# An attention chain beside projections: eight q buffers, the fourth q projection no longer behind all scores of the first key/value half, attention steps of 5.2

## The chip, the cores and the metric

One core of a Trainium2 chip runs the whole computation in one launch. The metric is the device time of that launch in microseconds (us). Engines: TensorE (PE, matmuls), VectorE (DVE), ScalarE (ACT), GpSimd (POOL), SyncE (SP, issues DMAs). Each engine runs its instructions in the order in which they are written, and waits on semaphores for the others.

## The reference

A two-layer encoder over 512 + 256 = 768 tokens of width 1024, all in fp32. Each layer is half a SwiGLU block, a mixer, half a SwiGLU block. The change lies in the mixer of layer 0, in short:

```
z = rmsnorm(x) @ w_in
u, vh = gelu(z[:, :1024]) split in two of 512
vh = layer_norm(vh)
vmix = per block of 128 tokens, per group of 128 columns: sgu_w[g] @ vh + sgu_b
a_out = u * vmix
q (8 heads of 64), k, v (2 heads of 64) = rest of z; rope on q and k
b_out = softmax over a window of 3 blocks of 128, with a sink, of q k^T / 8; times v
out = concat(a_out, b_out) @ w_out
```

Tokens of the two requests (4 and 2 blocks of 128) do not see each other. Four q heads share one k/v head.

## The kernel before, in words

Activations lie feature-major, in tiles of 128 features by 768 tokens, and every fp32 matmul is three passes: each operand is split into a high part (fp32r, ScalarE cast) and a low remainder (VectorE subtract, L115 for weights, L197 for activations), and TensorE adds high·high, high·low and low·high (`mm3`, L176). The mixer's tokens are worked on in two groups, 512 and 256 tokens wide (GROUPS). PSUM has four banks of the kind "mm" (projections) and four of the kind "aux" (attention, gate), each handed out in turn.

TensorE's order is written out by hand. The kernel keeps a model time `self.t` that each matmul advances by its nominal length. Side work is written as Python generators ("chains", `spawn`): a chain yields a gap, and is due again that much later in model time. After every `mm3`, `tick` steps the chains that are due, so side work is put between the matmuls of a projection. `run_until(cond)` (L164) is the other way to step them: it steps the chains in order of their due times, with no projection between, until the condition holds, moving the model time on. The orders of the other engines come from the framework's scheduler, which knows the dependences; it fixes them at build time.

In `mixer0` (L925), in the order of the code:

- the k and v projections, with rope tables and the split of k;
- the attention chain is spawned with the gap `GAP0` (L46);
- `q_heads(m)` for m = 0, 1, 2 (L996): each projects 128 q columns (two heads) in both groups, 8 `mm3` of 512 columns and 8 of 256, applies rope on VectorE (L960 to L963) and writes a high and a low tile for each group. Each group's tiles are taken from a ring of six buffers (tag q0, q1), that is, three calls' worth;
- `vh_part`: the gate half of the input projection, twice three blocks of 128 tokens, each 8 `mm3` of 512 columns. Each block's result goes through Gelu on ScalarE (L1119, which reads the PSUM bank) into a `sgu` chain: layer norm on VectorE (L1080, L1083, a reciprocal root in small integer and float steps L265 to L276, L1085, L1088, L1089), a split (vhh, vhl), then 12 small matmuls with the gate weights and an add (L1103);
- the line L1139, `self.run_until(lambda: (0, 5) in scored)`: the attention chain is stepped until it has issued the scores of half 0, block 5;
- `q_heads(3)`; the attention's half 1 needs q heads 2 and 3;
- `u_part` (L1121 and on): the u half, 4 times two groups, L1129, Gelu L1130, product L1133;
- `mixer_out`: the output projection; its operand tiles are split just ahead (oh on ScalarE L196, ol on VectorE L197).

The attention chain handles (half kv, block n) for kv = 0, 1 and n = 0 to 5. A round is: scores S of block n (12 matmuls; mask and row maximum on VectorE L905 and L909, exponentials on ScalarE L911, sink L915 to L917, reciprocal L918, scaling of p L920), a gap, values V of block n−1 (one pair of matmuls for each key block; moved out by L1049 and L1052), a gap, transposes T of p of block n (4 for each key block; split into th and tl), 0.3 of a gap. Blocks 0, 3, 4 and 5 have two key blocks, 1 and 2 three.

Weights come by DMA through four raw buffers (SP's queue), well ahead, and are split by ScalarE and VectorE.

Of the kernel before, what the change touches and what calls it, by code (L numbers as in the profile page):

```python
# [10 lines left out]
F32R = mybir.dt.float32r  # L11
# [5 lines left out]
P = 128  # L17
# [25 lines left out]

WTOTAL = 12 * D * FF + 8 * EARLY * P * D + D * 1792 + 2 * D * D + D * 3072 + D * 512
VTOK = (4.0,9.0)
GAP0 = 5.4  # L46
SGU = (8.0, 3.0, 4.0)
NP, NQ = 16, 2
GAPS1 = (3.5, 0.6, 3.5, 0.8)
# [2 lines left out]
class Trunk:  # L52
# [872 lines left out]
    def mixer0(self):  # L925
        nc = self.nc
        mp = self.mixer_open("m0")
# [29 lines left out]
        def roped(ps, c0, c1):  # L957
            n = c1 - c0
            t, u = tmp("rt")[:, :n], tmp("ru")[:, :n]
            nc.vector.stream_shuffle(out=u, in_=ps[:, :n], mask=swap)  # L960
            nc.vector.tensor_tensor(out=t, in0=ps[:, :n], in1=rct[:, c0:c1], op=ALU.mult)
            nc.vector.tensor_tensor(out=u, in0=u, in1=rst[:, c0:c1], op=ALU.mult)
            nc.vector.tensor_tensor(out=t, in0=t, in1=u, op=ALU.add)  # L963
            return t
# [18 lines left out]
        for g in (0, 1):  # L983
            c0, c1 = GROUPS[g]
# [11 lines left out]
        def q_heads(m):  # L996
            qs = []
            w = self.unit("l0_w_in", 0, KD, 1024 + m * P, P)
            for g in (0, 1):
                c0, c1 = GROUPS[g]  # L1000
                t = roped(self.proj(w, xs, GROUPS[g]), c0, c1)
                qs.append([mp.tile([P, c1 - c0], F32R, tag=f"q{g}", name=f"q{g}", bufs=6) for _ in "hl"])
                self.q_split(*qs[g], t)
            qheads.append(qs)

# [51 lines left out]
        qheads, scored, gates = [], [], []  # L1057

        def attention(gap):
            cur = None  # L1060
            for kv in (0, 1):
                for n in range(6):
                    while len(qheads) < 2 * kv + 2:
                        yield 0.5
                    new = score(kv, qheads[2 * kv : 2 * kv + 2], n)
                    scored.append((kv, n))
                    yield gap
                    if cur:
                        values(*cur[:3], tt)
                    yield gap  # L1070
                    cur = new
                    tt = turn(*cur)
                    yield 0.3 * gap
            yield 1.0
            values(*cur[:3], tt)
# [31 lines left out]
        def vh_part():  # L1107
            for n0 in (0, 3):
                ps = [self.psum() for _ in range(3)]
                for k in range(KD):  # L1110
                    if k % 2 == 0:
                        w = self.unit("l0_w_in", k, 2, 512, 512)
                    for i in range(3):
                        a, b = (n0 + i) * P, (n0 + i + 1) * P
                        st = (self.xh[k][:, a:b], self.xl[k][:, a:b])
                        self.mm3(ps[i], st, w[k % 2], k == 0, k == KD - 1)
                for i in range(3):
                    v = tmp("vg")
                    nc.scalar.activation(v, ps[i], AF.Gelu, scale=self.ry[:, n0 + i : n0 + i + 1])  # L1119
                    gates.append(self.spawn(sgu(n0 + i, v)))  # L1120
# [13 lines left out]

        att = self.spawn(attention(GAP0))
        for m in range(3):
            q_heads(m)
        vh_part()
        self.run_until(lambda: (0, 5) in scored)  # L1139
        q_heads(3)  # L1140
        u_part()
        self.mixer_out("l0_w_out", ot, att)
# [422 lines left out]
```

## Time and profile before

| | |
|---|---|
| median of 3 runs | 2632.54 us (2632.37 to 2633.5) |
| profiled execution, its own time | 2634.87 us |
| its span | 2633.1 us |
| its mean granted TensorE clock | 0.99 |
| first mixer in the span | about 535 to 740 us |

The profile is one execution. Its page gives busy times by engine, 40 slices of the span, and the chain of work that ended last. Further views are windows (busy time by engine and granted clock in each stretch), waits (what ended an engine's idle time, summed: total us, times, longest), and the timeline (start, duration, engine, line, operation, output<-inputs, shape; in brackets the idle time before it and what ended it). Matmuls are pipelined: their durations overlap, and the distance of their starts is what one costs.

### The profile page before, as it was taken

The numbers are of one execution on the slowest core, as the hardware profiler recorded it, in microseconds if no ns is written. First come the engines' busy times: TensorE is split into PE (matmuls) and PEld (weight loads), VectorE is DVE, ScalarE is ACT, GpSimd is POOL, SyncE is SP. The second block draws the span as 40 slices with busy tenths as digits, with TensorE's granted clock in tenths as the row PEclk, the third lists the DMA queues.
The fourth block names the chain that finished last, engine by engine and source line by source line (L and its number), as shares of the span: only waits on it lengthen the run. The fifth ranks groups of instructions, "written<-read, shape, count | busy, mean of one in ns | idle before, by whom it ended". The sixth has DMA issues, their size and how long they took to land.

```text
span 2633.1 us, 41175 instructions
## 1 busy us (share of the span) xinstructions
PE 2561.3 (97%) x15094; PEld 2491.3 (95%) x15094; DVE 2267.8 (86%) x4793; ACT 1365.6 (52%) x2851; POOL 88.0 (3%) x172
## 2 busy tenths in 40 slices
PE   7999999998999999999999999999999999999997
PEld 7999999987899999999999999989998989999997
DVE  8998889889779988898999888886777699988886
ACT  7544444555655544454654544454545465454443
POOL 0000000000100000000000000001222100000000
PEclk9999999999999999999999999999999999999998
DMA  5423222421223222222322222232221332222221
GB/s 168 133 78 103 71 81 65 145 87 37 89 77 97 81 81 77 68 75 86 96 81 81 73 73 74 88 111 63 63 63 40 105 104 81 81 71 74 68 87 54
DMA packets 83898, 218.99 MB, mean 83 GB/s; under 512 B 20080, under 2 KB 32880, under 8 KB 83696
## 3 DMA queue, kind: packets, MB, share of 16 engines
q1 hardware_dynamic: 83552, 216.34, 26.5%
q8 instruction: 118, 1.93, 0.3%
q14 instruction: 84, 0.69, 0.1%
q10 hardware_dynamic: 144, 0.03, 0.0%
HBM read 206.90 MB, written 15.07 MB: 84 GB/s over the span
## 4 chain that ended last, share of the span: by engine, by line
PE 86%; DVE 9%; ACT 2%; DMA 2%; issue 1%; SPq 0%; DVEq 0%; ACTq 0%
PE ps_mm L140 54%; PE ps_aux L140 31%; DMA raw<-in_w 1%; DVE wlo L115 1%; PE ps_aux L144 1%; DVE s L609 1%; DVE xl L739 1%; ACT p L911 1%; DVE p L920 0%; DVE p L905 0%; DVE tl L197 0%; ACT whi L114 0%; ACT xh L738 0%; DVE ol L197 0%; DVE x L706 0%
## 5 line engine op out<-in xcount | busy, mean ns | idle before, releaser
L114 ACT CAST whi<-s 128x512 fp32r<-128x512 f32 x496 | 304.9, 621 | 390.6 <-DVE s L609 133.1
L114 ACT CAST whi<-raw 128x512 fp32r<-128x512 f32 x512 | 311.0, 619 | 257.8 <-PE ps_mm L140 116.8
L115 DVE TENSOR_TENSOR wlo<-s,whi 128x512 fp32r<-128x512 f32 x496 | 337.0, 685 | 61.1 <-ACT whi L114 60.8
L115 DVE TENSOR_TENSOR wlo<-raw,whi 128x512 fp32r<-128x512 f32 x494 | 337.5, 691 | 28.3 <-ACT whi L114 24.1
L140 PE MATMUL ps_aux<-dt,whi 128*128 128x384 f32 x864 | 219.3, 334 | 2.1 <-ACT whi L114 2.1
L140 PE MATMUL ps_mm<-db,whi 128*128 128x384 f32 x864 | 219.2, 334 | 0.0
L140 PEld LDWEIGHTS ps_aux<-dt,whi 128*128 128x128 f32 x864 | 156.0, 188 | 2.4 <-ACT whi L114 2.4
L140 PEld LDWEIGHTS ps_mm<-db,whi 128*128 128x128 f32 x864 | 156.1, 188 | 0.0
L140 PE MATMUL ps_mm<-xh,whi 128*128 128x512 f32 (+1 forms) x416 | 147.4, 354 | 3.8 <-ACT xh L738 3.8
L140 PE MATMUL ps_aux<-dt,wlo 128*128 128x384 f32 x432 | 144.4, 334 | 0.3 <-DVE wlo L115 0.3
L140 PE MATMUL ps_mm<-db,wlo 128*128 128x384 f32 x432 | 144.4, 334 | 0.0
L140 PE MATMUL ps_mm<-xl,whi 128*128 128x512 f32 (+1 forms) x416 | 142.3, 342 | 1.1 <-DVE xl L739 1.1
L140 PE MATMUL ps_mm<-xh,wlo 128*128 128x512 f32 (+1 forms) x416 | 142.1, 341 | 0.0
L609 DVE TENSOR_TENSOR s<-raw 128x512 f32<-128x512 f32 x124 | 85.0, 686 | 23.0 <-DMA raw<-in_w 22.9
L499 DVE TENSOR_TENSOR u<-ps_aux,u 128x384 f32<-128x384 f32 x176 | 97.0, 551 | 2.8 <-PE ps_aux L140 2.6
L609 DVE TENSOR_TENSOR s<-raw,raw 128x512 f32<-128x512 f32 x124 | 83.7, 686 | 18.2 <-DMA raw<-in_w 18.0
L140 PE MATMUL ps_aux<-dh,whi 128*128 128x384 f32 x384 | 97.6, 335 | 0.6 <-DVE x L706 0.6
L911 ACT ACTIVATE p<-p,st 128x256 f32<-128x256 f32 (+3 forms) x144 | 68.9, 480 | 55.0 <-DVE st L909 54.9
L494 ACT COPY u<-ps_mm 128x384 f32<-128x384 f32 x176 | 83.5, 474 | 24.2 <-PE ps_mm L140 24.0
L661 DVE TENSOR_TENSOR x<-ps_aux,x 128x384 f32<-128x384 f32 x160 | 86.0, 552 | 9.3 <-PE ps_aux L140 9.2
L140 PEld LDWEIGHTS ps_mm<-xh,whi 128*128 128x128 f32 x416 | 79.9, 192 | 14.1 <-ACT xh L738 4.9
L140 PE MATMUL ps_mm<-oh,whi 128*128 128x384 f32 x256 | 88.1, 344 | 4.6 <-DVE x L888 4.0
(486 smaller groups left out, 8058.2 us busy)
## 6 DMA issues: line engine op xcount, KB each, us to landing
raw<-in_w SPq DMA_DIRECT2D x350, 512.0 KB, 3.7
xdm<-x SPq DMA_DIRECT2D x16, 384.0 KB, 2.3
x<-in_x SPq DMA_DIRECT2D x16, 192.0 KB, 5.5
x<-xdm SPq DMA_DIRECT2D x8, 384.0 KB, 3.4
xold<-xdm SPq DMA_DIRECT2D x8, 384.0 KB, 3.0
out_y<-y SPq DMA_DIRECT2D x8, 384.0 KB, 2.4
tab<-skew SPq DMA_DIRECT2D x8, 256.0 KB, 4.8
raw<-in_w SPq DMA_DIRECT2D x8, 256.0 KB, 2.6
```

The lines of the kernel that those rows point to most:

```text
L114: nc.scalar.copy(hi, src)
L115: (eng or nc.gpsimd).tensor_tensor(out=lo, in0=src, in1=hi.bitcast(F32), op=ALU.subtract)
L140: self.nc.tensor.matmul(out, lhsT=lhsT, rhs=rhs, start=start, stop=stop, **kw)
L144: self.nc.tensor.transpose(out, src, self.ident)
L494: nc.scalar.copy(e[n, out], bank[key, n])
L499: nc.vector.tensor_tensor(out=t, in0=bank[key, n], in1=t, op=ALU.add)
L609: f = lambda o, x, y, op: self.nc.vector.tensor_tensor(out=o, in0=x, in1=y, op=op)
L661: nc.vector.tensor_tensor(out=o, in0=ps, in1=o, op=ALU.add)
L739: nc.vector.scalar_tensor_tensor(out=lo, in0=src, scalar=gain, in1=hi.bitcast(F32), op0=ALU.mult, op1=ALU.subtract)
L911: nc.scalar.activation(outs[i], outs[i], AF.Exp, bias=nm[:, i : i + 1], accum_out=sm[:, i : i + 1])
```

## The change

Three edits, all for `mixer0`. Each attention step's gap is 5.2 instead of 5.4 model microseconds. The ring of q tiles has eight buffers for each group instead of six, so that the tiles of all four calls exist at once. The call of `run_until` ahead of `q_heads(3)` is gone, so that the fourth q projection follows the gate half directly, and the attention chain's steps fall between its matmuls and those of `u_part` as they come due.

```diff
-GAP0 = 5.4
+GAP0 = 5.2
...
-                qs.append([mp.tile([P, c1 - c0], F32R, tag=f"q{g}", name=f"q{g}", bufs=6) for _ in "hl"])
+                qs.append([mp.tile([P, c1 - c0], F32R, tag=f"q{g}", name=f"q{g}", bufs=8) for _ in "hl"])
...
         for m in range(3):
             q_heads(m)
         vh_part()
-        self.run_until(lambda: (0, 5) in scored)
         q_heads(3)
         u_part()
         self.mixer_out("l0_w_out", ot, att)
```

## The prediction

> **What bounds the kernel now.** I read the page first (busy times and the chain of waits), then the windows of the first mixer, then TensorE's waits there, then the timelines of TensorE, VectorE and ScalarE around the largest hole.
>
> ```profile
> span 2633.1 us, 41175 instructions
> PE 2561.3 (97%) x15094; PEld 2491.3 (95%) x15094; DVE 2267.8 (86%) x4793; ACT 1365.6 (52%) x2851; POOL 88.0 (3%) x172
> PE 86%; DVE 9%; ACT 2%; DMA 2%; issue 1%; SPq 0%; DVEq 0%; ACTq 0%
> ```
>
> TensorE carries the end: 97% busy, 86% of the chain. An edit that leaves its matmuls as they are can only move its idle time and the stretches that run at a low clock. VectorE at 86% is the only other engine near the path.
>
> The windows (columns: span, then busy time of PE, PEld, DVE, ACT, POOL, then the granted clock) show where in this mixer that time lies:
>
> ```profile
> 620.00:625.00 5.00, 0.18 (x1) 0.19 (x2) 5.00 (x38) 2.93 (x10) 0.00 (x0) 0.80 0.05 20
> 625.00:630.00 5.00, 3.91 (x20) 2.93 (x19) 5.00 (x13) 2.63 (x5) 0.00 (x0) 0.50 0.01 2
> 630.00:635.00 5.00, 5.00 (x22) 4.28 (x22) 4.88 (x28) 0.61 (x2) 0.00 (x0) 0.68 0.01 3
> 600.00:650.00 50.00, 41.87 (x252) 35.25 (x253) 48.44 (x191) 24.06 (x55) 0.00 (x0) 0.90 0.14 42
> 650.00:700.00 50.00, 48.67 (x296) 41.81 (x295) 38.93 (x114) 36.17 (x79) 2.58 (x2) 1.00 0.22 68
> ```
>
> TensorE does next to nothing from 620 to 625 and runs at a low clock until about 633, while VectorE is full. Behind 650 VectorE has 11 us of 50 to spare. The hole in the timeline:
>
> ```profile
> 617.56 0.39 PE L140 MATMUL ps_mm<-wlo,xh 128*128 128x512 f32 x1
> 617.79 0.39 PE L140 MATMUL ps_mm<-whi,xl 128*128 128x512 f32 x1
> ...
> 618.70 0.39 PE L140 MATMUL ps_aux<-tl,vt 128*128 128x512 f32 x1
> 624.82 2.03 PE L144 MATMUL ps_aux<-ident,p 128*128 128x128 f32 x8 [5.74 <-DVE p L920]
> ...
> 628.45 0.58 PE L140 MATMUL ps_aux<-kh,q 64*128 64x256 f32 x1 [1.09 <-DVE tl L197]
> ...
> 634.26 0.45 PE L140 MATMUL ps_mm<-xh,whi 128*128 128x512 f32 x1
> ...
> 645.06 0.28 PE L140 MATMUL ps_mm<-xh,whi 128*128 128x256 f32 x1
> 645.18 0.28 PE L140 MATMUL ps_mm<-xl,whi 128*128 128x256 f32 x1
> ```
>
> This is the place of the deleted line. Waiting for all scores of kv 0 lets the attention chain step with no projection between: values, transposes of block 4 (waiting 5.74 us for p), scores of block 5 (waiting 1.09 us for tl). At full clock a 512-column matmul follows the last by 0.23 us (617.56 to 617.79), a 256-column one by 0.12 (645.06 to 645.18). What holds p is VectorE's order, the gate's layer norm in front of it:
>
> ```profile
> 618.89 0.69 DVE L1080 BATCH_NORM_STATS2 bs<-vg 128x6 f32<-128x512 f32 x1
> ...
> 624.33 1.13 DVE L920 TENSOR_SCALAR p<-p,st 128x256 f32<-128x256 f32 x4
> ```
>
> **The change part by part.** The instructions are the same; their order differs. Durations come from the profiled execution (2634.87 us, span 2633.1), 2.3 us above the median of the runs, 2632.54; everything below is a difference inside that execution, and I add it to the median.
>
> *The wait that goes.* Between 619.09 (last matmul before the hole) and 634.26, 15.2 us, TensorE did 8 transposes, 12 score, 6 projection and 12 gate matmuls: 6 by 0.23 and 32 of at most 256 columns by 0.12 are 5.2 us at most, and about 4.7 since the score matmuls start in pairs. So 10.5 us are lost there (10.0 at least): 5.74 and 1.09 of waiting, the rest clock. Without the line the fourth q projection (24 matmuls of 512 columns by 0.23 and 24 of 256 by 0.12, 8.4 us) lies between the steps of blocks 4 and 5. Following the changed orders of both engines with the durations of before, I have p of block 4 ready at 629.2 and TensorE there at 631.8. −10.5 us. TensorE's other waits there (columns: total us, times, longest) are
>
> ```profile
> PE ps_aux L140 <- DVE vhl L197: 0.7, 2, 0.5
> PE ps_aux L140 <- DVE o L1103: 0.6, 1, 0.6
> ```
>
> and belong to the same stretch of the old order; what stands in their place is counted anew below: −1.3 us.
>
> *Eight q buffers.* The fourth projection would otherwise wait for the scores of kv 0 to release one of six; with eight it waits for none. It costs memory, no instruction: 0.
>
> *Steps of 5.2.* Each attention step issues one projection group (3 matmuls, 0.69 us) earlier. That changes ScalarE's order in the gate half. In the kernel before, all three gate Gelus come ahead of the exponentials:
>
> ```profile
> 586.28 0.69 ACT L1119 ACTIVATE vg<-ps_mm,sm 128x512 f32<-128x512 f32 x1
> 587.68 1.43 ACT L1119 ACTIVATE vg<-ps_mm,sm 128x512 f32<-128x512 f32 x2 [0.72 <-PE ps_mm L140]
> ...
> 589.64 1.28 ACT L911 ACT_TABLE_LOAD   x1
> 590.93 0.62 ACT L911 ACTIVATE p<-p,st 128x384 f32<-128x384 f32 x1
> ...
> 593.35 0.19 ACT L916 ACTIVATE st<-st 128x4 f32<-128x4 f32 x1
> ```
>
> In the changed order one gate Gelu comes, then a table load, four exponentials, another load, and only then the other two Gelus. The second of them frees the PSUM bank that TensorE takes at the matmul which now starts about
>
> ```profile
> 589.56 0.39 PE L140 MATMUL ps_mm<-whi,xh 128*128 128x512 f32 x1
> ```
>
> (same position in both orders). The first Gelu starts at 587.0 to 587.7 (behind its last matmul, which comes after the scores now), ends 0.7 later, then 1.28 for the load, 2.6 for exponentials and the sink's (590.93 to 593.54), 1.28 again, 0.7: 593.5 to 594.2. So TensorE waits 4.0 to 4.7 us where it waited nothing. Queued behind that matmul on TensorE are the values, the transposes and scores of block 3, all that feeds VectorE next.
>
> The next scores (block 3) then wait for tl of the transposes: in the changed VectorE order it stands behind the layer-norm steps of two gate blocks and reaches its end about 605.9, with TensorE there at 602 to 604, 2 to 4 us. The two waits replace lesser ones of before. Walking both engines with the row durations, TensorE ends the gate half at 623.3 instead of 618.0: +5.3 us.
>
> *The gate's mixing matmuls* of the second half now come beside the fourth q projection, whose rope work on VectorE is in front of their vhl. The first step of that rope is
>
> ```profile
> 642.96 0.74 DVE L960 STREAM_SHUFFLE ru<-ps_mm 128x512 f32<-128x512 f32 x1
> ```
>
> Four such steps and the q split for 512 columns are 3.1 us at some 0.62 each, and about half for 256. By the walk vhl of the first of two blocks is ready at 642.4 with TensorE there at 641.1, that of the next at 647.9 with TensorE at 645.1: 1.3 and 2.8 us, and a transpose bank of block 5 comes 0.7 late: +4.8 us.
>
> *Clock.* What a wait costs beyond itself:
>
> ```profile
> 2140.41 0.41 PE L140 MATMUL ps_mm<-b110h,whi 128*128 128x384 f32 x1 [2.70 <-DVE sg L508]
> 2142.00:2144.00 2.00, 2.00 (x8) 2.00 (x7) 1.45 (x4) 1.19 (x4) 0.00 (x0) 0.50 0.26 104
> 252.05 0.62 PE L140 MATMUL ps_aux<-dt,whi 128*128 128x384 f32 x2 [2.12 <-ACT whi L114]
> 254.00:256.00 2.00, 2.00 (x13) 2.00 (x12) 2.00 (x5) 0.07 (x1) 0.00 (x0) 1.00 0.00 0
> ```
>
> A wait of 2.70 is followed by a granted clock of 0.50 for about as long as the wait, so about half the wait again is lost; one of 2.12 leaves the clock at 1.00. The first new wait's clock loss falls into the second wait. The 2.8 at vhl sits on the edge: +1.3 us taken, 0 to 1.3. [...]
>
> *The end of the mixer.* The output projection follows the u projections; its operands oh and ol come two at a time, and the waits and casts of before are
>
> ```profile
> 690.41 0.38 PE L140 MATMUL ps_aux<-kh,q 64*128 64x256 f32 x1 [0.91 <-DVE tl L197]
> 701.24 0.44 PE L140 MATMUL ps_mm<-oh,whi 128*128 128x384 f32 x1 [0.58 <-ACT oh L196]
> 702.04 0.44 PE L140 MATMUL ps_mm<-ol,whi 128*128 128x384 f32 x1 [0.36 <-DVE ol L197]
> 691.97 2.58 ACT L196 CAST oh<-o 128x384 fp32r<-128x384 f32 x6 [0.54 <-PE ps_mm L140]
> 694.49 2.89 DVE L197 TENSOR_TENSOR ol<-o,oh 128x384 fp32r<-128x384 f32 x6
> ```
>
> 1.85 us, and with the shorter gaps around them about 3.0 in all. In the changed order the first output matmul waits for an ol behind more of the u product; then a pair of oh (0.43 each, 2.58 by 6) takes 0.86 and one of ol (0.48 each) 0.96 against some 0.51 for the three matmuls that use it (384 columns, 0.17 each between the two pitches above): I get 4.9 us lost, +2.0 (0 to 4). At the last values of the mixer, 45 matmuls (7.7 us) lie between them and their first reader, in the old order and the new; no cost. The weight loads on SP's queue keep their order, and none of them ends a wait of TensorE here: 0.
>
> *Table loads.* Before has 13 in this mixer (7, 4 and 2):
>
> ```profile
> L911 ACT ACT_TABLE_LOAD x7 | 9.0, 1283 | 0.1
> L1130 ACT ACT_TABLE_LOAD x4 | 5.1, 1283 | 0.1
> L1119 ACT ACT_TABLE_LOAD x2 | 2.6, 1283 | 0.0
> ```
>
> The changed order has 17. Four more by 1283 ns are 5.1 us on an engine that is about half busy; what of it is on the path is already in the walk of the gate half, the rest is hidden behind its idle time. [...]
>
> Sum: −10.5 −1.3 +5.3 +4.8 +1.3 +2.0 = +1.6 us, 2634. The bounds: with both waits of the gate half covered (0), those for vhl and their clock at half (3.1) and no loss at the end, −8.7: 2624. With the first wait's clock loss not covered by the second (+2) and the end at +4: 2638.
>
> **The rivals.** *Faster, 2624:* the hole goes and the new waits are mostly covered. For it: VectorE idles 11 us in 650 to 700, and the fourth projection is 8.4 us of work that doesn't need it at once. Against: VectorE is full from 620 to 630 and its work ahead of vhl isn't less. Price: the lower bounds above.
>
> *Slower, 2640:* ScalarE's switches starve VectorE. Between 600 and 650 VectorE idles 1.6 us; if the loads keep it from layer-norm statistics or p between 586 and 620, all that it owes later (p, tl, vhl) comes later by as much. Four loads of 1283 ns are 5.1 us, and with a half-clock stretch behind one wait of some 2.7 us (1.3) it is 2632.5 + 1.6 + 5.1 + 1.3 = 2640.5. It decides from about 3 us of VectorE idle in that stretch. For it: one Gelu stands ahead of each load. Against: before has VectorE full there with loads between too. [...]
>
> *Nothing moves, 2632.5:* VectorE's backlog to 650 sets the pace whatever TensorE's order; the hole is cut into pieces of the same sum.
>
> **How the numbers follow.** A measurement can tell about 0.2% (5.3 us) from no change: under 2627.3 is faster, above 2637.8 slower. My forecast gets 0.45 (of it 0.33 within, 0.05 faster, 0.07 slower), the faster rival 0.25 (0.22 beyond the bound, 0.03 within), the slower one 0.22 (all beyond), the one that moves nothing 0.08 (within). Faster 0.27, same 0.44, slower 0.29. The likeliest case alone ranges from 2628 to 2638; the range that takes in most of the rivals runs from 2622 to 2643.
>
> **What would show it.** Right: no TensorE wait over 1 us for p of block 4; a wait of 4 to 5 us near 590 for a PSUM bank held by ScalarE's Gelu, with a granted clock near 0.50 behind it; a wait for tl near 603; waits of 1 to 3 us for vhl near 642 and 647; 17 table loads. Wrong: no wait near 590 (then faster), or VectorE idle over 3 us from 586 to 620 (then slower), or the waits at the output projection more than 4 us above 3.0.

## The result and the profile after

The changed kernel takes 2638.86 us in the median of 18 runs (2635.36 to 2642.87), the kernel before 2634.22 in 18 (2631.38 to 2638.37) taken beside them. The ratio is 1.0019, with a 95% interval of 1.0012 to 1.0025: slower by 3 to 7 us, best 5.0. That lies inside the predicted range (2622 to 2643), above the forecast of 2634, and just within the 0.2% that the prediction called no change.

The page of the profiled execution after (2637.11 us) is nearly that of before: TensorE is 97% busy and has 88% of the chain.

```profile
span 2635.3 us, 41188 instructions
PE 2562.6 (97%) x15094; PEld 2491.5 (95%) x15094; DVE 2269.9 (86%) x4793; ACT 1371.4 (52%) x2855; POOL 89.5 (3%) x172
PE 88%; DVE 8%; ACT 2%; issue 1%; DMA 1%; SPq 0%; DVEq 0%; ACTq 0%
```

Single executions of one kernel differ by some microseconds (2631.38 to 2638.37 in 18 runs of the kernel before), so I read the mixer alone, from TensorE's first v transposes to its first wait for x at L888, and in it the last matmul of the gate half. In the kernel before (first fence) and after (second), in TensorE's timeline:

```profile
542.77 0.60 PE L144 MATMUL ps_aux<-ident,vf 128*128 128x128 f32 x4
763.61 0.44 PE L140 MATMUL ps_mm<-oh,whi 128*128 128x384 f32 x1 [0.21 <-DVE x L888]
```

```profile
543.61 0.60 PE L144 MATMUL ps_aux<-ident,vf 128*128 128x128 f32 x4
...
594.23 0.69 PE L140 MATMUL ps_mm<-whi,xh 128*128 128x512 f32 x1 [3.94 <-ACT vg L1119]
...
607.09 0.38 PE L140 MATMUL ps_aux<-kh,q 64*128 64x256 f32 x1 [1.85 <-DVE tl L197]
...
626.19 0.40 PE L140 MATMUL ps_mm<-whi,xl 128*128 128x512 f32 x1
...
646.25 0.33 PE L140 MATMUL ps_aux<-swh,vhl 128*128 128x128 f32 x1 [1.04 <-DVE vhl L197]
650.08 0.33 PE L140 MATMUL ps_aux<-swh,vhh 128*128 128x128 f32 x1 [1.06 <-ACT vhh L196]
651.65 0.33 PE L140 MATMUL ps_aux<-swh,vhl 128*128 128x128 f32 x1 [1.13 <-DVE vhl L197]
...
697.34 0.69 PE L140 MATMUL ps_mm<-ol,whi 128*128 128x384 f32 x1 [2.71 <-DVE ol L197]
...
769.29 0.44 PE L140 MATMUL ps_mm<-oh,whi 128*128 128x384 f32 x1 [0.23 <-DVE x L888]
```

The mixer takes 220.84 us before (763.61 − 542.77) and 225.68 after: +4.84, close to the measured difference of the runs (4.6 between the medians, 5.0 by the ratio). It splits in two. The gate half ends 75.02 us behind the transposes before (617.79 − 542.77) and 82.58 after: +7.56. From there to the end it is 145.82 before and 143.10 after: −2.72. This points to a removed line that pays and to steps of 5.2 that cost more than it pays; the experiments test that.

In ScalarE's timeline after, one gate Gelu, a load, the exponentials, a load, and two Gelus stand where the prediction put them:

```profile
587.58 0.69 ACT L1119 ACTIVATE vg<-ps_mm,sm 128x512 f32<-128x512 f32 x1 [0.73 <-PE ps_mm L140]
588.29 1.28 ACT L911 ACT_TABLE_LOAD   x1
589.58 0.62 ACT L911 ACTIVATE p<-p,st 128x384 f32<-128x384 f32 x1
...
592.20 1.28 ACT L1119 ACT_TABLE_LOAD   x1
593.49 1.27 ACT L1119 ACTIVATE vg<-ps_mm,sm 128x512 f32<-128x512 f32 x2
```

Windows of the kernel after (clock in the third number from the right): behind each of the two waits of the gate half the clock is at 0.50 for 3.4 us, and it is full between them. The last two lines take the gate half and what follows it as a whole.

```profile
590.97:594.38 3.41, 0.15 (x1) 0.15 (x2) 3.13 (x12) 3.38 (x8) 0.00 (x0) 1.00 0.12 49
594.38:597.79 3.41, 3.41 (x9) 2.67 (x10) 3.41 (x11) 2.02 (x4) 0.00 (x0) 0.50 0.00 0
597.79:604.62 6.83, 6.83 (x38) 5.73 (x36) 6.71 (x37) 1.83 (x3) 0.00 (x0) 1.00 0.26 77
604.62:608.03 3.41, 1.56 (x15) 0.99 (x13) 3.41 (x7) 2.18 (x4) 0.00 (x0) 1.00 0.29 71
608.03:611.44 3.41, 3.41 (x9) 2.73 (x9) 3.25 (x13) 0.62 (x1) 0.00 (x0) 0.50 0.23 90
585.00:618.00 33.00, 27.08 (x133) 21.73 (x132) 28.18 (x107) 20.39 (x40) 0.00 (x0) 0.90 0.21 64
618.00:650.00 32.00, 29.56 (x178) 24.39 (x176) 30.71 (x121) 19.30 (x39) 0.00 (x0) 1.00 0.05 17
```

The same two long windows before:

```profile
585.00:618.00 33.00, 31.63 (x182) 25.85 (x180) 32.69 (x127) 21.75 (x44) 0.00 (x0) 1.00 0.21 64
618.00:650.00 32.00, 24.67 (x144) 20.68 (x143) 30.64 (x127) 14.29 (x35) 0.00 (x0) 0.84 0.06 18
```

VectorE loses 4.5 us of work in the gate half (28.18 against 32.69), and does as much as before behind it. What it waited for there, in its own waits of 585 to 650 after, is ScalarE:

```profile
DVE wlo L115 <- ACT whi L114: 2.5, 2, 2.0
DVE st L917 <- ACT st L916: 2.0, 1, 2.0
```

### The profile page after: what moved, and what is told of

The parts are those of the page before. It is cut to its first block, busy times and chain, and to the rows that moved or that the text cites. A ratio compares the mean times of both kernels' runs of the same rounds, so it can differ in the third digit from the quotient of the medians.

```text
span 2635.3 us, 41188 instructions
## 1 busy us (share of the span) xinstructions
PE 2562.6 (97%) x15094; PEld 2491.5 (95%) x15094; DVE 2269.9 (86%) x4793; ACT 1371.4 (52%) x2855; POOL 89.5 (3%) x172
## 4 chain that ended last, share of the span: by engine, by line
PE 88%; DVE 8%; ACT 2%; issue 1%; DMA 1%; SPq 0%; DVEq 0%; ACTq 0%
PE ps_mm L140 55%; PE ps_aux L140 32%; DVE wlo L115 1%; PE ps_aux L144 1%; DMA raw<-in_w 1%; DVE xl L739 1%; DVE p L905 0%; ACT p L911 0%; ACT whi L114 0%; DVE p L920 0%; DVE ol L197 0%; DVE s L609 0%; DVE tl L197 0%; ACT xh L738 0%; DVE x L706 0%
## 5 line engine op out<-in xcount | busy, mean ns | idle before, releaser
L115 DVE TENSOR_TENSOR wlo<-s,whi 128x512 fp32r<-128x512 f32 x496 | 336.4, 684 | 65.4 <-ACT whi L114 65.1
L115 DVE TENSOR_TENSOR wlo<-raw,whi 128x512 fp32r<-128x512 f32 x494 | 336.6, 688 | 25.0 <-ACT whi L114 21.0
```

The source lines that it names most:

```text
L115: (eng or nc.gpsimd).tensor_tensor(out=lo, in0=src, in1=hi.bitcast(F32), op=ALU.subtract)
```

## The experiments

The theory to test (A): the change is two effects, a loss in the gate half that belongs to the steps of 5.2 through ScalarE's order, and a gain behind it that belongs to the removed line. The rival (B): VectorE's backlog sets the pace, and TensorE's waits only change place. All kernels in one table: "gate" and "mixer" read as above, from one profiled execution each; "half clock" is the time in the mixer at a granted clock of 0.50; ratios have their 95% interval against the kernel before on the same chip. The mixer of e2 and e3, whose waits agree, differs by 0.7 us, and the clock is at 0.50 for 3.4 us more in e3, so smaller differences of "mixer" say nothing. The gate half holds the same number of matmuls in all kernels but two: in e4 some 20 attention matmuls fall behind it, and in e12 the fourth q projection (8.4 us) falls ahead of its end.

| kernel | gate half ends | mixer | half clock | ratio |
|---|---|---|---|---|
| before | 75.02 | 220.84 | 10.2 | 1 |
| the change | 82.58 | 225.68 | 13.7 | 1.0019 (1.0012 to 1.0025) |
| e1_gap_only | 80.98 | 230.65 | 20.5 | 1.0038 (1.0025 to 1.0050) |
| e2_free54 | 75.01 | 219.71 | 10.2 | 0.9999 (0.9990 to 1.0008) |
| e3_free54_b6 | 75.02 | 220.39 | 13.7 | 1.0002 (0.9993 to 1.0011) |
| e4_free58 | 73.05 | 227.60 | 17.1 | 1.0030 (1.0019 to 1.0041) |
| e5_after_shift | 75.41 | 220.77 | 10.2 | 1.0001 (0.9992 to 1.0010) |
| e6_free54_late_gate | 75.00 | 222.37 | 13.7 | 1.0007 (0.9998 to 1.0016) |
| e7_free54_out45 | 75.01 | 222.49 | 13.7 | 1.0005 (0.9995 to 1.0014) |
| e8_free54_both | 74.99 | 222.65 | 17.1 | 0.9998 (0.9989 to 1.0008) |
| e9_before_pool | 82.06 | 227.87 | 17.1 | 1.0040 (1.0027 to 1.0054) |
| e10_free54_pool | 83.69 | 229.06 | 20.5 | 1.0040 (1.0027 to 1.0053) |
| e11_after_pool | 85.39 | 229.41 | 17.1 | 1.0039 (1.0026 to 1.0052) |
| e12_q3_first | 84.88 | 228.27 | 20.5 | 1.0030 (1.0019 to 1.0040) |

**The steps of 5.2 alone (e1).** Diff against the kernel before:

```diff
-GAP0 = 5.4
+GAP0 = 5.2
```

> Attention steps of 5.2 alone; six q buffers and the wait for all scores of half 0 stay. Theory A (the steps of 5.2 set ScalarE's order of one gate Gelu, load, four exponentials, load, two Gelus, and this alone costs the gate half about 5 us): the wait of about 3.9 us near 594 for vg is there, as is one of 1 to 2 us for tl near 607; the hole before block 4's transposes stays above 4 us; 2637 to 2640 where before has 2633, ratio about 1.002. Rival B (VectorE's backlog sets the pace, so a wait near 594 only shortens the hole later): the hole falls to 1 to 2 us and the time is that of before within 1 us.

Measured: median 2643.6 (2641.4 to 2643.95), ratio 1.0038, more than either theory said. TensorE's waits from 582 to 712:

```profile
PE ps_aux L144 <- DVE p L920: 5.1, 1, 5.1
PE ps_mm L140 <- ACT vg L1119: 3.9, 1, 3.9
PE ps_aux L140 <- DVE vhl L197: 3.2, 2, 3.0
```

The wait for vg is the same 3.9 us as in the change, so it belongs to the steps. The hole stayed (5.1 of 5.7): time lost ahead of it did not shorten it, against B. The wait for tl near 607 was 0.54, not 1 to 2, and a wait for vhl of 3.0, which the expectation did not have, came on top.

**The removed line without the steps (e2), and with six buffers (e3).** Diff of e2 against the kernel before; e3 is the same without the first pair of lines:

```diff
-tag=f"q{g}", name=f"q{g}", bufs=6
+tag=f"q{g}", name=f"q{g}", bufs=8
...
-        self.run_until(lambda: (0, 5) in scored)
```

> The wait for all scores of half 0 removed and eight q buffers, attention steps still 5.4. Theory A: all three gate Gelus stand together again, no wait over 0.5 us near 590, gate half ends as before (618), the hole of 5.7 and its low clock (10.5 us) are gone; what remains are waits for vhl (1 to 3 us) and for ol at the output projection (2 to 3 us): 2626 to 2629 where before has 2633, ratio about 0.998. Rival B (the fourth projection's rope work ahead of vhl costs what the hole cost): 2633 to 2638, with waits for vhl of 4 us and more.

> As e2_free54 with six q buffers. Theory A: the fourth projection's q writes wait on ScalarE and VectorE until block 5's scores of half 0 have read the first heads; th, vhh and exponentials queue behind them; 1 to 4 us more than e2_free54. Rival: the scheduler writes q late enough that nothing waits, equal to e2_free54 within 1 us, so that eight buffers buy nothing.

Measured for e2: 2633.2 (2630.41 to 2636.09), no difference; the mixer is 1.1 us shorter. The gate half is as before (75.01), and in e1 it is not, so the steps alone move it. The hole is gone, but its 10.5 us are not won. TensorE's timeline of e2 has what stands in its place:

```profile
643.75 0.33 PE L140 MATMUL ps_aux<-swh,vhl 128*128 128x128 f32 x1 [3.04 <-DVE vhl L197]
...
689.99 0.69 PE L140 MATMUL ps_mm<-oh,whi 128*128 128x384 f32 x1 [3.45 <-ACT oh L196]
```

They are followed by 3.4 and 6.8 us at half clock. From the gate half's end to the mixer's, TensorE waits 9.5 us before and 8.2 in e2, and the clock is at 0.50 for 10.2 us in either: most of what the hole cost is there again. B's size for these waits (4 us and more for vhl) was too large, but its sum was right, A's was not. e3: 2632.22 (2631.31 to 2638.05): the intervals of e2 and e3 overlap over nearly their whole length. At steps of 5.4 eight buffers buy nothing that these runs can tell from six.

**Other steps (e4).** `GAP0 = 5.8` in the changed kernel.

> The changed kernel with steps of 5.8 instead of 5.2: attention is spread further, 11 table loads in this mixer instead of 17. Theory A: no wait near 594, fewer loads, but the last blocks of attention come later: the waits for ol at the output projection decide; 2624 to 2630 if they stay below 3 us. Rival: attention's last values come too late for the last output steps (more than 3 us of wait there), 2630 to 2636.

Measured 2641.43 (2640.09 to 2642.29). There are fewer table loads (11), but the last block of attention came late and TensorE waited elsewhere: 5.01 us for a PSUM bank read at L1052, and 4.37 us for p near the end of the output projection:

```profile
640.26 0.45 PE L140 MATMUL ps_aux<-swh,vhh 128*128 128x128 f32 x1 [5.01 <-DVE o L1052]
...
745.32 2.02 PE L144 MATMUL ps_aux<-ident,p 128*128 128x128 f32 x8 [4.37 <-DVE p L920]
```

The rival stated for this run holds in sign, at a larger size than it gave.

**One projection group later (e5).** Against the changed kernel:

```diff
-                    yield 0.3 * gap
+                    yield 0.3 * gap + 0.7 * ((kv, n) == (0, 1))
```

> The changed kernel, steps of 5.2, with 0.7 model us more after the transposes of block 1, so that the scores of block 2 come one projection group later and ScalarE's order has the three gate Gelus together again. Theory A (the 3.94 us wait for vg and all behind it in the gate half come from that order alone): no wait over 0.5 us from 588 to 612, the gate half ends about 75 us behind the mixer's first v transposes instead of 82.6, the mixer (from those to the first wait for x at L888, 225.7 in the changed kernel, 220.8 before) takes 219 to 221, the time 2631 to 2634. Rival B (VectorE's backlog): the gate half ends earlier but the waits for vhl and the output operands grow by as much, mixer 224 to 226, 2637 to 2639.

Measured 2634.42 (2631.44 to 2636.21), ratio 1.0001; the gate half ends at 75.41, the mixer takes 220.77, 4.9 us less than in the change. This, with e1, shows the cause of the change's loss: with the steps still 5.2 us apart, putting block 2's scores one group later (and all later steps with them) puts ScalarE's three Gelus together again, the wait for vg is gone, and so is the whole loss. But the 7.2 us won in the gate half come out as 4.9 at the end: a wait for vhl of 4.32 stands behind it in place of three of 1.0 to 1.1, and half clock lasts 6.8 us behind it, where it was 3.4 behind those three. A's figures for the gate half and the mixer hold and the time is 0.4 above its range, but two waits over 0.5 us are left between 588 and 612 (1.50 for vhh, 0.89 for wlo), against A; B's mechanism shows behind the gate half.

**Moving the two remaining waits (e6 to e8).** e6, against e2:

```diff
-            yield SGU[2]
+            yield SGU[2] + 4.0 * (n >= 3)
```

> e2_free54 (no wait for all scores, steps 5.4) with the gate's 12 small matmuls of blocks 3 to 5 issued 4 model us later. If the 3.04 us wait for vhl and its low clock in e2_free54 are a matter of place: they go, the mixer falls from 219.7 to 215 to 216, time about 4 us below e2_free54. If they stand for VectorE work that must be done before the u products anyway: the wait comes back at the output projection (oh, 3.45 us there before, 5 to 7 then) and the mixer stays within 1.5 us of 219.7.

e7, against e2 (in the output projection of this mixer):

```diff
-        for k in early:
+        for k in early if cols else (4, 5, 0, 1, 2, 3):
             ready(k)
...
+            if m == 0 and not cols:
+                pss = [self.proj(w, src, HALVES[h], ks=(4, 5, 0, 1, 2), last=False) for h in (0, 1)]
+                for h in (0, 1):
+                    put(m, h, self.proj(w, src, HALVES[h], ps=pss[h], ks=(3,), first=False))
+                continue
```

> e2_free54 with the output projection's first two groups summed over k = 4, 5, 0, 1, 2 first and k = 3 last, and the operand splits in that order (4 and 5 come from attention's half 0 and are long done). If the 3.45 us wait for oh and its low clock are latency of the last u product alone (table load, four exponentials, load, Gelu, product, split): they go or fall below 1 us, mixer 214 to 216, time about 4 to 5 us below e2_free54. If ScalarE or VectorE as a whole is late there: the wait only moves to a later k and the mixer stays within 1.5 us of 219.7.

e8 has both.

> e6 and e7 in one kernel. If both losses are of place and latency they add up: mixer 210 to 212, time 2624 to 2626 where before has 2633, ratio about 0.997: then it is the removed line's 10 us that shows at last. If VectorE's total sets the pace: within 2 us of the better of e6 and e7.

None of them is faster: 2634.39, 2633.42 and 2633.95. In the profiled executions the mixer is 2.7 to 2.9 us longer than in e2, which neither branch of e6 and e7 had (e8 lies within 2 us of them, as its second branch said), with 3.4 to 6.8 us more at half clock; the times of the runs can't be told from that of the kernel before. The waits moved (e6 first, then e7), in e6 to p and not to oh:

```profile
643.46 0.74 PE L144 MATMUL ps_aux<-ident,p 128*128 128x128 f32 x2 [3.46 <-DVE p L920]
...
646.39 1.08 PE L144 MATMUL ps_aux<-ident,p 128*128 128x128 f32 x4 [1.30 <-DVE o L1052]
```

```profile
692.15 0.69 PE L140 MATMUL ps_mm<-oh,whi 128*128 128x384 f32 x1 [5.47 <-ACT oh L196]
```

In e6 the wait for p ends 100.8 us behind the first v transposes (643.46 − 542.71); in e2 the wait for vhl ended at 100.6 (643.75 − 543.17). In e7 the wait for oh ends at 147.0 (692.15 − 545.16), in e2 at 146.8. Both suggest that TensorE's order decides which operand it waits for, not when VectorE and ScalarE are through.

**VectorE's total (e9 to e11).** The subtractions for the gate half's weights go to GpSimd; the same edit on the kernel before, e2 and the change:

```diff
-                        w = self.unit("l0_w_in", k, 2, 512, 512)
+                        w = self.unit("l0_w_in", k, 2, 512, 512, nc.gpsimd)
```

(`unit` hands the engine to the subtraction at L115.)

> The kernel before, with the low parts (wlo) of the gate half's weights made on GpSimd instead of VectorE: 16 subtractions, 0.6 us each on VectorE, 1.34 each on GpSimd (its mean for the same shape elsewhere). Theory C (formed after the runs so far: VectorE, full from 585 to 650 in every kernel with steps of 5.4, sets the pace of this stretch): some 6 to 9 us of VectorE work leave it; the hole before block 4's transposes shrinks from 5.7 to under 1.5 us though no order of TensorE is changed, the mixer falls from 220.8 to 213 to 216 and the time by 5 to 7 us. Theory A (the hole comes from the order that the removed line writes): the hole stays above 4 us and the mixer within 2 us of 220.8.

> e2_free54 (no wait for all scores, steps 5.4) with the same subtractions on GpSimd. Theory C: the 3.04 us wait for vhl and its low clock go, the mixer falls from 219.7 by 4 to 7 us to 213 to 216, close to e9_before_pool, since what both lacked was VectorE time. Theory A: the removed line's 10 us shows over e9_before_pool. If GpSimd's longer subtraction holds up TensorE (waits for wlo in the gate half), both lose the same there.

> The changed kernel with the same subtractions on GpSimd. The wait of 3.9 us for vg near 594 is ScalarE's order and stays; behind it, Theory C says VectorE has caught up and the waits for tl near 607 and vhl near 646 to 652 (4 us in all) go below 1 us: mixer from 225.7 to 217 to 220, still 3 to 5 us above e10_free54_pool, which is what the steps of 5.2 cost. If those waits stay, VectorE's total isn't what they stand for.

All three are about 0.4% slower, outside every time that was expected. Two conditions held: in e9 the hole stayed above 4 us (5.19, Theory A), and in e11 the waits for vg (3.96) and for vhl and vhh (1.04, 1.07 and 1.13) stayed. The loss is in and ahead of the gate half (it ends at 82 to 85). From its end to the mixer's end they take 145.81, 145.37 and 144.02, beside 145.82, 144.70 and 143.10 of the same kernels without the edit. Windows from the first v transposes to the gate half's end (before, then e9), and of e9's last 13 us ahead of that end:

```profile
542.77:617.79 75.02, 73.43 (x423) 61.19 (x421) 68.16 (x221) 42.65 (x91) 0.00 (x0) 1.00 0.26 78
```

```profile
545.29:627.35 82.06, 76.96 (x423) 62.87 (x422) 70.57 (x207) 42.52 (x91) 22.45 (x16) 0.96 0.24 72
614.00:627.35 13.35, 13.35 (x90) 11.54 (x89) 11.16 (x36) 8.17 (x19) 0.00 (x0) 1.00 0.17 46
```

The expectation counted only the work that leaves VectorE. Sixteen subtractions of 0.68 us (10.9 us) are gone from it, yet it is busy 2.4 us longer (70.57 against 68.16). A step that starts beside one of GpSimd's subtractions took 1.72 us where it took 0.69 before (the step of L963 before, then rows of e9):

```profile
554.58 0.69 DVE L963 TENSOR_TENSOR rt<-rt,ru 128x512 f32<-128x512 f32 x1
```

```profile
556.53 1.29 POOL L115 TENSOR_TENSOR wlo<-raw,whi 128x512 fp32r<-128x512 f32 x1 [5.49 <-ACT whi L114]
556.65 1.72 DVE L963 TENSOR_TENSOR rt<-rt,ru 128x512 f32<-128x512 f32 x1
```

So the move took nothing off VectorE here, and TensorE waited more for tl, p and o (1.5, 2.0 and 0.8 us from 543 to 630, where it waited 0.2, 0 and 0.6 in the gate half before). Which of those waits comes from longer steps is left open, since the edit also makes wlo later and changes the scheduler's orders. What it does tell: the hole is there nearly unchanged (5.19 us for p), though VectorE has 2.2 us to spare in the last 13.35 ahead of the gate half's end (0.07 before), so the hole doesn't come from VectorE work carried over from the gate half. It is made at the gate half's end.

**The fourth projection ahead of the gate half (e12).** Against e2:

```diff
-        for m in range(3):
+        for m in range(4):
             q_heads(m)
         vh_part()
-        q_heads(3)
```

> Eight q buffers, steps of 5.4, no wait for all scores, and all four q projections ahead of the gate half. Theory D (formed after e9 to e11: the losses behind the gate half are VectorE's queue of that place, three layer norms that start at its end with the fourth projection's rope work among them, and not its total before): with the rope work (4.7 us) ahead of the gate half, the 3 us wait for vhl behind it falls below 1.5 us, the stretch from the gate half's end to the mixer's end, less the 8.4 us projection that has moved, is 2 to 5 us shorter than in e2_free54 (144.7, so 132 to 134), mixer 214 to 218, time 2628 to 2631. Rival (a queue of fixed length: u projections come sooner behind the gate and wait for its results instead, at vhl or at the u product): waits of 4 us or more for vhl or for p behind the gate half, mixer 219 to 223, time 2632 to 2636.

Measured 2640.22 (2639.13 to 2643.02). The stretch from the gate half's end to the mixer's takes 143.4 us, where Theory D had 132 to 134. The wait did not fall; vhh and vhl now take 2.88 and 1.69, a wait of 2.08 for a bank that L1052 reads follows, and the clock is at 0.50 for 17 us:

```profile
642.20 0.33 PE L140 MATMUL ps_aux<-swh,vhh 128*128 128x128 f32 x1 [2.88 <-ACT vhh L196]
644.32 0.47 PE L140 MATMUL ps_aux<-swh,vhl 128*128 128x128 f32 x1 [1.69 <-DVE vhl L197]
```

```profile
644.14:661.21 17.07, 14.81 (x67) 13.75 (x68) 13.97 (x55) 7.74 (x16) 0.00 (x0) 0.50 0.00 1
```

The last gate matmul comes 27.0 us behind the gate half's end (111.85 − 84.88), as in e2 (27.0), e3 (27.5), e7 (27.5), e10 (27.0), e11 (27.1) and the change (26.8); in the others it is 28 to 32, but for e9 (23.5). The rival holds in kind (the mixer, 228.27, and the time lie above its ranges, which had no such stretch of half clock). e2 and e12 fit a queue on VectorE and ScalarE behind the gate half whose length hardly depends on where the fourth projection stands; that is argued from these two, not shown by itself. In the kernel before the last gate matmul comes 23.4 us behind, with the hole inside and the fourth projection for the most part after it.

No version of these twelve is measurably faster than the kernel before.

## Why the prediction was right, and where it was not

By its own steps, in microseconds:

| step | predicted | measured |
|---|---|---|
| the hole and the small waits at its place | −11.8 | gone: no wait for p of block 4 |
| the wait for vg | 4.0 to 4.7 | 3.94 |
| the next wait for tl | 2 to 4 | 1.85 |
| gate half's end | +5.3 | +7.56 |
| waits for vhl and vhh | 1.3 + 2.8 | 1.04 + 1.06 + 1.13 |
| a bank for block 5 | 0.7 (its transposes) | 0.25 (its scores, for o, L1052) |
| waits at the output projection | 4.9 for 3.0 | 2.9 for 2.0, and 3.4 us of half clock behind |
| from the gate half's end to the mixer's | −3.7 | −2.72 |
| sum | +1.6 | +4.84 |

*The direction* was right: a gain behind the gate half, a larger loss in it, from the order of Gelus and exponentials that the steps of 5.2 bring. e1, e2 and e5 show it by parts: the steps cost 9.8 us of mixer with the line in place (e1) and 6.0 without (the change against e2); the line's removal gives 1.1 at steps of 5.4 and 5.0 at 5.2. The eight buffers at 0 were right in size, but not for the reason given: in e3, at steps of 5.4, six do as well.

*The step that was mis-sized is the clock.* The prediction read a low clock "for about as long as the wait", said that the first wait's clock loss "falls into the second wait", and put none for the second. In the gate half the waits grew from 1.23 us (0.16, 0.28, 0.23 and 0.56 in the timeline before) to 5.95 (3.94, 1.85 and 0.16), by 4.72, less than the 5.3 of the sum; the other 2.8 of the 7.56 are two stretches at 0.50, from 594.38 to 597.79 and from 608.03 to 611.44. At 0.50 a 512-column matmul follows the last by 0.43 us (595.14 to 595.57), at full clock by 0.23 (598.21 to 598.44). The first stretch ends over 7 us before the second wait begins, so nothing of it is covered. The second wait, 1.85, should by the prediction's bracket (2.12 and 2.70) have left the clock alone, and has a stretch of its own. The low clock behind the prediction's own wait of 2.70 lasts 3.41 us (2141.90 to 2145.31), not 2.70. Behind the gate half the waits fell from 9.5 us to 6.6, by 3.0, and the stretch by 2.7. Half clock there went from 10.2 us to 6.8, but 2.9 of the 10.2 lay inside waits, so what it cost stayed nearly what it was (half of 7.3, then half of 6.3), where the prediction let 2.4 of it go.

*The cover.* The prediction gave −10.5 for the removed line and counted new waits against it. That sum held within 1 us. What it had not seen is that these waits can be the hole in other places: in e2, e6, e7 and e8 a wait for vhl, p or oh came whatever TensorE was given to do. The case called "nothing moves" (0.08) was the nearest description of the removed line at steps of 5.4.

*The slower rival* named VectorE kept idle by ScalarE between 586 and 620, deciding from 3 us. VectorE did: it idles 4.9 of the 34 us from 586 to 620 after, 0.3 before. So the prediction's own sign for "then slower" came true, beside most of its signs for being right. It was this mechanism in part that set the result between forecast and rival; e5, which restores the order, gives back 4.9 us of mixer and a full VectorE (32.76 of 33 us):

```profile
585.00:618.00 33.00, 30.26 (x180) 24.89 (x180) 32.76 (x127) 20.95 (x44) 0.00 (x0) 1.00 0.20 64
```

On the loads: the change has 17, e5 again 13, but e5 also restores Gelus' order, so the loads' own price was not measured apart. In the change the exponential starts (589.58) at the end of its load (588.29 + 1.28), as before (590.93, behind the load of 589.64).

## What to carry to other kernels

A large hole in the bound engine's timeline is worth only what the engine it waits for can do earlier: ask whether the queue behind that operand gets shorter, or whether another operand of the same queue is next. In a hand-written order a shift of one small group can change another engine's order at an operation that shares a scarce bank; look for which order each engine gets, not only for the edited one. And price a new wait together with the clock behind it: where the clock fell in the two profiled executions, that was 3.41 us at 0.50 (behind the waits of 1.85 and 3.94 alike) or a multiple (10.2 us at the hole), and not a share of the wait.

## What the runs showed of the hardware that was not expected

In these profiles the clock's answer to a short wait isn't a function of its length. Outside the change, where both kernels run the same instructions, a wait of 2.12 us (252.05 before, 251.33 after) left the clock at 1.00 in 254 to 256 before, and in the profile after the same window reads

```profile
254.00:256.00 2.00, 2.00 (x8) 2.00 (x8) 1.16 (x2) 0.00 (x0) 0.00 (x0) 0.50 0.00 0
```

The other way round, the wait for sg of 2.70 at 2140.41, followed by 0.50 before, is 2.89 after and followed by full clock:

```profile
2145.16 0.41 PE L140 MATMUL ps_mm<-b110h,whi 128*128 128x384 f32 x1 [2.89 <-DVE sg L508]
```

```profile
2146.00:2152.00 6.00, 6.00 (x36) 6.00 (x35) 5.86 (x12) 4.31 (x10) 0.00 (x0) 1.00 0.58 169
```

So the wait of 2.12 us was followed by 0.50 in one execution and not in the other, and so was the wait for sg (2.70 and 2.89).

The windows show where the clock changes. In the profile after, the stretches at 0.50 from 200 to 800 us begin at 253.04, 594.38, 608.03, 652.40 and 696.78 and last 3.41 us each. The distances of their starts, 341.34, 13.65, 44.37 and 44.38 us, are 100, 4, 13 and 13 times 3.413. In the profile before, those from 600 to 2300 us begin at 622.97, 1766.44, 2141.90 and 2220.41, which are 335, 110 and 23 times 3.413 apart. Each lasts a whole number of such steps: one for each of the five after, three for the one at the hole before (622.97 to 633.21); the one of e12 (644.14 to 661.21) lasts five.

Cut at these steps, the windows give TensorE's idle time in each. After, most of the wait of 2.12 and a shorter one behind it (0.33) lie in one step (249.63 to 253.05, TensorE idle 2.02 of it), which is followed by 0.50. Before, it falls on two, the second (250.92 to 254.33) idle for 1.46, and the clock stays full. The wait of 2.89 splits into 1.75 and 1.13 and leaves it full too; that of 2.70 has 1.92 in one step (2138.49 to 2141.90), which is followed by 0.50. No exact bound follows: in the profile before, one step with 1.62 idle (2217.00 to 2220.41) is followed by 0.50, and the 1.75 after is not. What sets the clock beyond these figures was not shown.

In the kernels with subtractions on GpSimd, some of VectorE's steps took longer. In e9 the rope step L963 at 556.65 took 1.72 us instead of 0.69; it starts inside GpSimd's subtraction of 556.53 to 557.82. The six steps of L1088 from 585 to 650 took 852 ns in the mean in e9, 853 in e10 and 845 in e11, where before has 680. Those of L1089 in the same stretch kept theirs (680, 681 and 688 beside 682), so not each step was longer. Why some were was not shown.
